# Retention's v, k and y turned by VectorE in 32x32 blocks and put in place by DMA through DRAM, in one layer of a hybrid encoder

## The chip, the core and the metric

The kernel runs on one core of a Trainium2 chip. A core has a tensor engine (PE, with its weight loads shown apart as PEld), VectorE (DVE), ScalarE (ACT), GpSimd (POOL) and SyncE (SP), which issues most transfers, and 16 DMA engines. The metric is the device time of one execution in microseconds, as the median of several runs; less is better.

## The reference

```
h = rms_norm(x)                                  # x: 1024 x 2048, float32
rq, rk, rv, rg, aq, ak, av, ag = split(h @ w_in) # w_in: 2048 x 6656
# retention, 8 heads x 128, per head, in chunks of C = 128 tokens:
q, k = rotary(rq), rotary(rk) * 128**-0.5
scores = (q_c @ k_c.T) * decay                   # within a chunk
inner  = scores @ v_c
kv_c   = (k_c * k_dec).T @ v_c                   # "outer products", 128 x 128
state  = state * chunk_decay + kv_c              # scan over the chunks
cross  = (q_c * q_dec) @ state_before_c
y = inner + cross, forward scan plus backward scan
y = (y - mean) * rsqrt(var + eps) * gn_w + gn_b  # per head, over its 128 columns
y_ret = y * silu(rg)
y_att = window_attention(aq, ak, av) * silu(ag)
out = rms_norm(x + concat(y_ret, y_att) @ w_out)
```

## The kernel before

All of it is float32. The input projection is computed transposed (channels on partitions, tokens along the row) by a two-by-two block scheme with seven products instead of eight, each product a sum of three matmuls on operands split into a high and a low half (lines 98, 99 and 100; matmuls of 128x512). The low half of the weights (`wL`) is made on DVE and the high half (`wH`) on ACT, one product ahead. Finished tiles of 128 channels by 1024 tokens go to DRAM, into `pr`.

The other work runs beside the projection as background jobs: generators that `advance()` moves on by one piece, a step, after every six matmuls of the projection. First attention, then retention head by head, then the gating, beside which the output projection starts. `idle(n)` lets a job rest n steps; `needs` waits until blocks of the projection are done. PE, SP and POOL execute in the order in which the program is written, with this interleaving; the order on DVE and ACT is chosen by a planner.

A retention head: `kT` and `qT` (channels on partitions) are fetched from `pr` with rotary on DVE; scores on PE (line 787); `vT` is fetched (line 761). `transposed()` (line 542) turns a 128x1024 tile by two groups of four 128x128 transposes on PE, each a matmul with `ident`, into PSUM. It is used three times a head: v and k come out as tokens on partitions, copied by ACT to `v_tok` (line 797) and `k_tok` (line 803), and y, normalised on DVE (line 891) with tokens on partitions, is turned back to channels, where ACT multiplies by gn_w and adds gn_b (line 899) before it is stored to `mix` (line 905). `vd` is v scaled by both decays (line 808). The outer products (line 820) take `k_tok` as the stationary and `vd` as the moving operand. The states are split into `sH` and `sL`, 14 pairs of 128x128, for the cross term. The gating loads `mix` and the gate on ACT's queue, three tiles ahead (lines 1280, 1281), and multiplies after Silu.

Stores and small buffers come from rotating pools: `ct` (128x512, 8 buffers), `ax` for results in PSUM. SP's DMAs share eight semaphores, so that at most eight of its transfers are on their way.

Of the kernel before, what the change touches and what calls it, by code (L numbers as in the profile page):

```python
# [17 lines left out]

P = 128
S = 1024  # L20
D = 2048
# [16 lines left out]
M = 4  # L38
# [19 lines left out]
def hybrid_layer_kernel(  # L58
# [80 lines left out]
    pr = [dram.tile([P, S], F32, name=f"pr{i}") for i in range(52)]  # L139
    mix = [dram.tile([P, S], F32, name=f"mix{i}") for i in range(KT)]  # L140

    rows_d = dram.tile([1, HALF], F32, name="rows_d")
# [579 lines left out]


    def retention():
        with right("ret") as ret:
# [4 lines left out]
            busy = set()  # L730
            kq, vs = {}, {}
            rot = ret.tile([P, 2, S], F32, name="rot")
            HP = P // 2

            def fetch(name, c, h):

                t = ret.tile([P, S], F32, name=name, tag=name)
                nc.sync.dma_start(out=t, in_=pr[c + h])
                beside = []

                def pair(i):
                    beside.append(ret.tile([P, HALF], F32, name="rx", tag="sd" if h == 0 and c == T_RQ else "rx", bufs=2))
                    for r in (0, HP):
                        nc.sync.dma_start(out=beside[i][r:r + HP], in_=pr[c + h][HP - r:P - r, half(i)])

                for i in range(2):
                    pair(i)
                yield from idle(7 if h or c == T_RK else 11)
                for i in range(2):
                    u, b = t[:, half(i)], beside[i]  # L750
                    behind(h == 0, nc.vector.tensor_tensor(out=u, in0=u, in1=rot[:, 0, half(i)], op=ALU.mult))
                    yield
                    behind(h == 0, nc.vector.tensor_tensor(out=b, in0=b, in1=rot[:, 1, half(i)], op=ALU.mult))
                    add(u, u, b)
                    yield
                kq[name, h] = t

            def fetch_v(h):
                yield from needs("rv" + str(h // 4))
                t = ret.tile([P, S], F32, name="vT", tag="vdq")  # L760
                nc.sync.dma_start(out=t, in_=pr[T_RV + h])
                yield from idle(5)
                vs[h] = t

            def next_of(name, c, h):
# [6 lines left out]
            def head(h):  # L772
# [10 lines left out]
                for b in range(2):  # L783
                    sc = ax()
                    for t in range(4):
# [5 lines left out]
                                            in1=dT.rearrange("p (o e) -> p o e", o=1).broadcast_to([P, 4, P]), op=ALU.mult)  # L791
                    sds.append(sd)
                while h not in vs:
                    yield
                v = ret.tile([P, NT, P], F32, name="v_tok")
                for b, pt in transposed(vs.pop(h)):
                    nc.scalar.copy(out=v[:, 4 * b:4 * b + 4], in_=chunks(pt))
                    yield
                while busy:
                    yield  # L800
                k_tok = ret.tile([P, NT, P], F32, name="k_tok", tag="y")
                for b, pt in transposed(kT):
                    nc.scalar.copy(out=k_tok[:, 4 * b:4 * b + 4], in_=chunks(pt))
                    yield
                start(next_of("kT", T_RK, h + 1))
                vd = ret.tile([P, NT, 2, P], F32, name="vd", tag="vdq")
                for d in range(2):
                    nc.scalar.mul(vd[:, :, d], v, kd[:, d * RH + h:d * RH + h + 1])
                yield from idle(3)

                sH, sL = (ret.tile([P, 2 * NT - 2, P], F32R, name="s" + c) for c in "HL")
                prev = None
                def outer(i0):
                    kvp = ax()
                    todo = []
                    for i in range(i0, min(i0 + 2, NT - 1)):
                        for d in range(2):
                            c, to = (NT - 1 - i, NT - 2 - i) if d else (i, i + 1)
                            p = kvp[:, blk(len(todo))]
                            nc.tensor.matmul(p, k_tok[:, c], vd[:, c, d], start=True, stop=True)  # L820
                            todo.append((i, d, to, p))
# [4 lines left out]
                for i0 in range(2, NT + 2, 2):  # L826
                    todo, ahead = ahead, (outer(i0) if i0 < NT else None)
                    for i, d, to, p in todo:
# [4 lines left out]
                        else:  # L833
                            nc.vector.scalar_tensor_tensor(out=cur[:, d], in0=prev[:, d], scalar=cd[:, d * RH + h:d * RH + h + 1],  # L834
                                                           in1=p, op0=ALU.mult, op1=ALU.add)
                        split(sH[:, 2 * to + d - 1], sL[:, 2 * to + d - 1], cur[:, d])
                        if d == 1:
                            prev = cur
                    yield
# [9 lines left out]
                def cross(c0):  # L849
                    cr = ax().rearrange("p (c d e) -> p c d e", d=2, e=P)  # L850
                    for t in range(2):
                        c = c0 + t
                        lo, hi = (1 if c == 0 else 0), (1 if c == NT - 1 else 2)
                        mm3(cr[:, t, lo:hi], qH[:, blk(c)], qL[:, blk(c)], *(s[:, 2 * c + lo - 1:2 * c + hi - 1] for s in (sH, sL)))
                    yield
# [8 lines left out]
                def inner(b):  # L864
                    yi = ax()
                    for t in range(4):
                        nc.tensor.matmul(yi[:, blk(t)], sds[b][:, t], v[:, 4 * b + t], start=True, stop=True)  # L867
                    nc.scalar.copy(out=y[:, 4 * b:4 * b + 4], in_=chunks(yi))
# [11 lines left out]
            def normed(h, y, bn, mv):  # L880
# [7 lines left out]
                nc.gpsimd.tensor_tensor(out=rs, in0=rs, in1=neg_half, op=ALU.pow)  # L888
                yield from idle(2)
                for c in range(NT):  # L890
                    nc.vector.tensor_scalar(out=y[:, c], in0=y[:, c], scalar1=mv[:, c, 0:1], scalar2=rs[:, c:c + 1],
                                            op0=ALU.subtract, op1=ALU.mult)
                    if c % 4 == 3:
                        yield
                yield from idle(2)
                outs = []
                for b, pt in transposed(y.rearrange("p c e -> p (c e)")):
                    yo = ct()
                    nc.scalar.activation(out=yo, in_=pt, func=AF.Identity, scale=gw[:, h:h + 1], bias=gb[:, h:h + 1])
                    outs.append((mix[h][:, half(b)], yo))  # L900
                    yield
                busy.discard(h)
                yield
                for dst, yo in outs:
                    nc.sync.dma_start(out=dst, in_=yo)
                finished.add(h)
# [224 lines left out]
    def on_done(p, b):  # L1131
        if b in done:
            since.setdefault(b, clock[0])
        if p == 1 and b == "akv":
            start(attention())
        if p == 2 and b == "rq1":
            start(residual())
# [109 lines left out]
    def gating():  # L1247
# [13 lines left out]
        def operand_tiles(part, gates):  # L1261
# [6 lines left out]
            def mix_in():  # L1268
                d, g = todo.popleft()
                nc.scalar.activation(out=g, in_=g, func=AF.Silu)  # L1270
                nc.vector.tensor_tensor(out=d, in0=d, in1=g, op=ALU.mult)
                mixed.append(d)

            def gate():
                for s in range(2):
                    yield from needs(gates[s])
                    for i in range(s * M, (s + 1) * M):
                        t = (RH if part == 0 else 0) + i
                        d, g = src[:, s, i % M], places[i % 3]
                        behind(True, nc.scalar.dma_start(out=d, in_=mix[t]))  # L1280
                        behind(True, nc.scalar.dma_start(out=g, in_=pr[T_RG + t if t < RH else T_AG + t - RH]))
                        todo.append((d, g))
                        yield
# [243 lines left out]
```

## Time and profile before

| | |
|---|---|
| median of 3 runs | 1525.29 us (1524.96 to 1526.89) |
| profiled execution, span | 1524.4 us (no other time of this execution is recorded) |
| PE / DVE / ACT / POOL busy | 99% / 71% / 45% / 10% |
| DMA moved | 310.53 MB, mean 204 GB/s |
| packets | 153352, of which 13697 under 512 bytes |

The span is from the first to the last recorded instruction. Busy shares are averages over stages of the program; matmuls overlap each other, so a matmul's duration is longer than the distance from one start to the next. In rows of groups, the two numbers behind the bar are the busy time in us and the mean duration of one in ns, and the number behind the next bar is the idle time of the engine just before them, with what ended it. In rows of DMA issues the last numbers are the size and the median time from issue to landing.

### The profile page before, as it was taken

How to read it: one execution, taken by the hardware profiler on the slowest of the kernel's cores; microseconds unless marked ns; L12 is line 12 of the kernel's file. 1: busy time of each engine (PE TensorE's matmuls, PEld its weight loads, DVE VectorE, ACT ScalarE, POOL GpSimd, SP SyncE). 2: the span in 40 equal slices, each digit the busy share in tenths (PEclk: the TensorE clock that was granted, in tenths of full speed). 3: DMA queues.
4: the chain of work that ended last, by engine and by line, in shares of the span. 5: the costliest groups of instructions: out<-in, count | busy, mean ns of one | idle time of the engine just before them, and what ended most of it. 6: DMA issues, size and time to landing. Idle time of an engine off the chain costs nothing.

```text
span 1524.4 us, 20497 instructions
## 1 busy us (share of the span) xinstructions
PE 1510.5 (99%) x7406; PEld 1274.0 (84%) x7406; DVE 1088.3 (71%) x1943; ACT 686.6 (45%) x1139; POOL 151.0 (10%) x169
## 2 busy tenths in 40 slices
PE   9999999999999999999999999999999999999997
PEld 7888888788888888888888888888888888888886
DVE  6896594557767575756977797779755966776766
ACT  7543462234545454533445444543444643542425
POOL 0000001111010000011212000001211102020001
PEclk9999999999999999999999999999999999999999
DMA  8288847889573424796677655488689679395756
GB/s 319 68 277 316 311 166 193 222 207 251 163 204 128 138 80 167 281 315 156 139 179 205 196 174 193 152 297 299 157 207 262 152 217 251 85 212 162 219 177 251
DMA packets 153352, 310.53 MB, mean 204 GB/s; under 512 B 13697, under 2 KB 72481, under 8 KB 144418
## 3 DMA queue, kind: packets, MB, share of 16 engines
q1 hardware_dynamic: 128050, 254.15, 49.1%
q0 software_dynamic: 19728, 36.71, 15.6%
q10 hardware_dynamic: 5472, 18.36, 3.5%
q8 instruction: 58, 0.95, 0.3%
q14 instruction: 44, 0.36, 0.1%
HBM read 193.03 MB, written 124.52 MB: 208 GB/s over the span
## 4 chain that ended last, share of the span: by engine, by line
PE 84%; issue 9%; DMA 4%; DVE 2%; POOL 0%; ACT 0%; SPq 0%; ACTq 0%; POOLq 0%; DVEq 0%
PE pj L100 21%; PE pj L98 21%; PE pj L99 21%; PE ax L99 5%; PE ax L100 5%; PE ax L98 5%; PE ax L820 2%; PE ax L542 1%; DMA xt<-in_x_dram 1%; PE ax L619 1%; DMA pr<-ct 1%; PE ax L787 1%; PE ax L867 1%; DMA yt<-pr 1%; DVE wL L84 0%
## 5 line engine op out<-in xcount | busy, mean ns | idle before, releaser
L98 PE MATMUL pj<-c,wH 128*128 128x512 f32 x1444 | 576.8, 399 | 0.0
L100 PE MATMUL pj<-c,wL 128*128 128x512 f32 x1440 | 562.6, 391 | 1.6 <-DVE wL L84 1.6
L99 PE MATMUL pj<-c,wH 128*128 128x512 f32 x1444 | 563.0, 390 | 0.0
L100 PEld LDWEIGHTS pj<-c,wL 128*128 128x128 f32 x1440 | 270.3, 188 | 60.7 <-DVE wL L84 2.5
L98 PEld LDWEIGHTS pj<-c,wH 128*128 128x128 f32 x1444 | 271.6, 188 | 49.7 <-ACT ct L292 0.4
L99 PEld LDWEIGHTS pj<-c,wH 128*128 128x128 f32 x1444 | 271.8, 188 | 49.5 <-DVE c L948 0.2
L87 ACT CAST wH<-a 128x1024 fp32r<-128x1024 f32 (+1 forms) x159 | 166.3, 1046 | 250.2 <-PE pj L99 138.0
L84 DVE TENSOR_TENSOR wL<-a,wH 128x1024 fp32r<-128x1024 f32 x157 | 191.9, 1222 | 109.4 <-ACT wH L87 105.9
L292 ACT COPY ct<-pj 128x512 f32<-128x512 f32 x192 | 111.1, 584 | 220.3 <-PE pj L100 219.7
L262 POOL DMA_DIRECT2D pr<-ct x104 | 92.2, 961 | 612.9 <-DVE ct L91 474.6
L91 DVE TENSOR_TENSOR ct<-pj,ct 128x512 f32<-128x512 f32 x164 | 109.1, 688 | 58.9 <-PE pj L100 58.0
L84 DVE TENSOR_TENSOR wL<-s,wH 128x1024 fp32r<-128x1024 f32 x56 | 68.4, 1222 | 89.8 <-ACT wH L87 89.4
L99 PE MATMUL pj<-wL,c 128*128 128x512 f32 x224 | 87.3, 390 | 0.0
L100 PE MATMUL pj<-wH,c 128*128 128x512 f32 x224 | 87.2, 389 | 0.0
L98 PE MATMUL pj<-wH,c 128*128 128x512 f32 x224 | 87.1, 389 | 0.0
L99 PE MATMUL ax<-wL,c 128*128 128x512 f32 x208 | 81.2, 390 | 0.4 <-DVE wL L84 0.4
L100 PE MATMUL ax<-wH,c 128*128 128x512 f32 x208 | 80.9, 389 | 0.0
L98 PE MATMUL ax<-wH,c 128*128 128x512 f32 x208 | 80.9, 389 | 0.0
L87 ACT CAST wH<-s 128x1024 fp32r<-128x1024 f32 x56 | 59.1, 1055 | 16.4 <-PE ax L100 8.8
L87 ACT CAST sH<-st 128x128 fp32r<-128x128 f32 x112 | 29.9, 298 | 46.9 <-DVE st L834 29.2
L99 PEld LDWEIGHTS pj<-wL,c 128*128 128x128 f32 x224 | 42.0, 188 | 8.9 <-DVE wL L84 0.3
L98 PEld LDWEIGHTS pj<-wH,c 128*128 128x128 f32 x224 | 42.0, 188 | 8.8
(243 smaller groups left out, 2057.7 us busy)
## 6 DMA issues: line engine op xcount, KB each, us to landing
a<-in_w_in_dram SPq DMA_DIRECT2D x103, 512.0 KB, 5.8
kept<-c SPq DMA_DIRECT2D x28, 1024.0 KB, 7.3
c<-kept SPq DMA_DIRECT2D x28, 1024.0 KB, 9.9
pr<-ct SPq DMA_DIRECT2D x110, 256.0 KB, 5.4
pr<-ct POOLq DMA_DIRECT2D x104, 256.0 KB, 6.2
a<-in_w_out_dram SPq DMA_DIRECT2D x18, 512.0 KB, 5.4
rx<-pr SPq DMA_DIRECT2D x64, 128.0 KB, 3.8
ysrc<-mix ACTq DMA_DIRECT2D x16, 512.0 KB, 5.4
```

Of the source, the lines that this page charges most:

```text
L84: return nc.vector.tensor_tensor(out=dst, in0=src, in1=high.bitcast(F32), op=ALU.subtract)
L87: behind(pinned, nc.scalar.copy(out=dst_h, in_=src))
L91: nc.vector.tensor_tensor(out=dst, in0=a, in1=b, op=ALU.add)
L98: nc.tensor.matmul(po, aH, bH, start=first, stop=False, **kw)
L99: nc.tensor.matmul(po, aH, bL, start=False, stop=False, **kw)
L100: nc.tensor.matmul(po, aL, bH, start=False, stop=last, **kw)
L262: nc.gpsimd.dma_start(out=dst, in_=t, accum_op=ALU.add)
L292: nc.scalar.copy(out=t, in_=bank)
L542: nc.tensor.transpose(pt[:, blk(t)], src[:, blk(b * 4 + t)], ident)
L619: nc.tensor.transpose(pt[:, blk(j)], s[:, blk(j)], ident)
L787: nc.tensor.matmul(sc[:, blk(t)], kT[:, c], qT[:, c], start=True, stop=True)
L820: nc.tensor.matmul(p, k_tok[:, c], vd[:, c, d], start=True, stop=True)
```

## The change

VectorE has a transpose that turns each 32x32 block of a tile in its place. Three helpers use it: `turn_half` (a 128x512 half of v), `turn_pair` (half of y), and a call in the fetch of `kT`. The block positions are put right by a trip through DRAM: the turned tile is stored, and `gather` reads it back by four DMAs of 32 partitions each, in runs of 512 bytes for v (`vz` to `v_tok`), 256 bytes for k (`kz` to `k_tok`) and 1024 bytes for y (`mix`, read in the gating). So:

- v: a job `turn_v`, started after v's projection or one head ahead, loads a half, turns it on DVE and stores it; `fetch_v` gathers. v's columns come in four runs of 32 per chunk, which the later instructions read through an access pattern; `vd` takes four ACT instructions instead of two.
- k: turned after rotary, stored to `kz`, gathered by `fetch_k_tok`. `k_tok` holds two chunks with their columns interleaved, so that the outer product's stationary operand is read with a step of two elements.
- y: normalised by ACT (scale and bias by token) in place of DVE, turned on DVE, stored to `mix`; gn_w and gn_b are applied in the gating, where retention's tiles are gathered by SP.
- apart from this, the states' split takes both directions in one instruction: 7 pairs of 128x256 in place of 14 of 128x128.

```diff
+    def turn_pair(dst, src, pair):
+        nc.vector.transpose(out=dst.rearrange("p (b c i) -> p b c i", b=2, i=SQ),
+                            in_=src.rearrange("p (c b i) -> p b c i", b=NB, i=SQ)[:, 2 * pair:2 * pair + 2])
+    def gather(dst, src):
...
+        for b in range(NB):
+            nc.sync.dma_start(out=dst[b * SQ:(b + 1) * SQ].rearrange("p (n r) -> p n r", r=of.shape[-1]), in_=of[b])
...
+    def turn_v(h):
+        yield from needs("rv" + str(h // 4))
+        for m in range(2):
+            f, z = ct(), ct()
+            nc.sync.dma_start(out=f, in_=pr[T_RV + h][:, half(m)])
+            yield from idle(6)
+            turn_half(z, f)
+            yield
+            nc.sync.dma_start(out=vz[h][m], in_=z)
+            yield
...
+                    if c == T_RK:
+                        zs.append(ct())
+                        for n in range(2):
+                            nc.vector.transpose(out=chunks2(zs[i])[:, n].rearrange("p (b j c) -> p c b j", b=NB, c=2),
+                                                in_=chunks2(u)[:, n].rearrange("p (c b i) -> p c b i", b=NB, c=2))
...
+                start(fetch_k_tok(h))
...
-                for b, pt in transposed(vs.pop(h)):
-                    nc.scalar.copy(out=v[:, 4 * b:4 * b + 4], in_=chunks(pt))
...
-                for b, pt in transposed(kT):
-                    nc.scalar.copy(out=k_tok[:, 4 * b:4 * b + 4], in_=chunks(pt))
...
-                            nc.tensor.matmul(p, k_tok[:, c], vd[:, c, d], start=True, stop=True)
+                            nc.tensor.matmul(p, k_tok[:, c // 2, :, c % 2], vd[:, c, d], start=True, stop=True)
...
-                        split(sH[:, 2 * to + d - 1], sL[:, 2 * to + d - 1], cur[:, d])
                         if d == 1:
+                            both = slice(i, 2 * NT - 2 - i, 2 * NT - 3 - 2 * i)
+                            split(sH[:, both], sL[:, both], cur)
...
-                    nc.vector.tensor_scalar(out=y[:, c], in0=y[:, c], scalar1=mv[:, c, 0:1], scalar2=rs[:, c:c + 1],
-                                            op0=ALU.subtract, op1=ALU.mult)
+                    nc.scalar.activation(out=y[:, c], in_=y[:, c], func=AF.Identity, scale=rs[:, c:c + 1], bias=mv[:, c, 0:1])
...
-                for b, pt in transposed(y.rearrange("p c e -> p (c e)")):
...
+                for b in range(2):
+                    zs.append(ct())
+                    turn_pair(zs[b], y.rearrange("p c e -> p (c e)"), b)
...
+                if t < RH:
+                    nc.scalar.activation(out=e, in_=e, func=AF.Identity, scale=gw[:, t:t + 1], bias=gb[:, t:t + 1])
...
+                        if t < RH:
+                            gather(e, mix[t])
```

The order on PE around the scores of the fourth head (head 3), before: `c` and `wH`, `wL` are the projection's operands, and each row is one instruction or, with x4, four alike.

```order
L787 MATMUL ax<-qT,kT 128x128 x4
L542 MATMUL ax<-ident,y 128x128 x4
L98 MATMUL pj<-c_5644,wH 128x512
L99 MATMUL pj<-c_5644,wH 128x512
L100 MATMUL pj<-c_5644,wL 128x512
L98 MATMUL pj<-c_5644,wH 128x512
L99 MATMUL pj<-c_5644,wH 128x512
L100 MATMUL pj<-c_5644,wL 128x512
L542 MATMUL ax<-ident,vT 128x128 x4
L98 MATMUL pj<-c_5644,wH 128x512
```

And at the same place in the changed kernel (its lines are numbered anew: 99 to 101 are the projection, 850 the scores):

```order
L850 MATMUL ax<-qT,kT 128x128 x4
L99 MATMUL pj<-c_5863,wH 128x512
L100 MATMUL pj<-c_5863,wH 128x512
L101 MATMUL pj<-c_5863,wL 128x512
L99 MATMUL pj<-c_5863,wH 128x512
L100 MATMUL pj<-c_5863,wH 128x512
L101 MATMUL pj<-c_5863,wL 128x512
L850 MATMUL ax<-qT,kT 128x128 x4
L99 MATMUL pj<-c_5863,wH 128x512
```

The two groups with `ident` between the projection's sixes, of y of the head before and of v, are gone; the scores and the sixes stay.

The order on SP from the fetch of qT of head 2 to that of the next kT, before. `a` are weights of the projection, `res` the residual, `mix` the results of head 1.

```order
L738 DMA qT<-pr_67 128x1024
L744 DMA rx<-pr_67 64x512 x4
L1153 DMA res_240<-in_x_dram 16x16384
L761 DMA vT<-pr_83 128x1024
L171 DMA a_7337<-in_w_in_dram 128x4x256
L1153 DMA res_241<-in_x_dram 16x16384
L171 DMA a_7393<-in_w_in_dram 128x4x256
L171 DMA a_7395<-in_w_in_dram 128x4x256
L905 DMA mix_118<-ct 128x512 x2
L738 DMA kT<-pr_76 128x1024
```

The changed kernel, from the same fetch of qT (its `rx`) to the gather of k (`vz_143`, `kz_135`: head 2's v and k on their way through DRAM):

```order
L789 DMA rx<-pr_67 64x512 x4
L765 DMA vz_143<-ct 128x512
L1215 DMA res_257<-in_x_dram 16x16384
L202 DMA a_7307<-in_w_in_dram 128x4x256
L202 DMA a_7309<-in_w_in_dram 128x4x256
L808 DMA kz_135<-ct 128x2x256 x2
L164 DMA v_tok<-vz_143 32x8x128 x4
L202 DMA a_7452<-in_w_in_dram 128x4x256
L965 DMA mix_118<-ct 128x512 x2
L1215 DMA res_258<-in_x_dram 16x16384
L761 DMA ct<-pr_84 128x512
L164 DMA k_tok<-kz_135 32x16x64 x4
```

The load of vT has become loads and stores of halves and a gather of four DMAs, and the store of k and its gather have come in; k's gather stands behind the stores of `mix`, whose data comes from DVE's transpose of y of head 1. In steps of the program: v's gather stands 8 steps ahead of the scaling to `vd` and 5 behind the store of v's second half (in the first head 2 steps behind it), k's gather 9 behind its store and 6 ahead of the outer products. A head takes 27 steps in place of 28, the first outer product of the first head stands 12 steps later, and the gating of retention's part starts 2 steps later.

95 lines of the change are left out of this document (64 added, 31 removed).

## The prediction

> **What bounds the kernel now.** I read first the page's busy times, then the waits of the tensor engine, then the busy times of the stretches with retention in them.
>
> ```profile
> span 1524.4 us, 20497 instructions
> ...
> PE 1510.5 (99%) x7406; PEld 1274.0 (84%) x7406; DVE 1088.3 (71%) x1943; ACT 686.6 (45%) x1139; POOL 151.0 (10%) x169
> ```
>
> PE is busy for 1510.5 of 1524.4 us. This is one profiled execution, whose span lies 0.9 us under the median of the three runs (1525.3), so I add differences to 1525.3. Next, whether PE waits for anything that the change touches:
>
> ```profile
> PE pj L100 <- DVE wL L84: 1.6, 2, 0.9
> PE pj L1086 <- POOL ident masks.py:199: 1.4, 1, 1.4
> ...
> PE ax L99 <- DVE wL L84: 0.4, 1, 0.4
> ```
>
> These are the largest waits of the whole run, with their total, count and longest: under 5 us together, and nothing in them belongs to v, k or y. So PE's own list of work sets the end: work taken from it shortens the run by its full length, as long as the other engines and the transfers keep up with a shorter list. How much room they have shows in two stretches, the middle of retention (four heads long) and the end of it (heads 6 and 7), where the projection also reads its kept input back from DRAM. The columns are window, length, PE, weight loads, DVE, ACT, POOL (each with its instructions), granted clock, DMA share, GB/s:
>
> ```profile
> 801.00:1003.00 202.00, 202.00 (x1104) 173.79 (x1103) 161.14 (x384) 91.69 (x164) 16.68 (x13) 1.00 0.61 186
> 1003.00:1075.00 72.00, 72.00 (x392) 61.70 (x391) 51.81 (x116) 33.61 (x57) 6.10 (x4) 1.00 0.93 324
> ```
>
> A head lasts 202/4 = 50.5 us, with 40.3 us of DVE, 22.9 us of ACT, and DMA at 61%. In the last stretch DMA is at 93%. DVE and, at the end, DMA are what could come next; the clock is 1.00 in both.
>
> **Part 1: 192 transposes leave PE.** The price of one group of four, between the projection's matmuls (start, duration, engine, line):
>
> ```profile
> 760.22 0.39 PE L99 MATMUL pj<-c,wH 128*128 128x512 f32 x1
> 760.44 0.39 PE L100 MATMUL pj<-c,wL 128*128 128x512 f32 x1
> 760.67 0.39 PE L98 MATMUL pj<-c,wH 128*128 128x512 f32 x1
> 760.90 0.39 PE L99 MATMUL pj<-c,wH 128*128 128x512 f32 x1
> 761.12 0.39 PE L100 MATMUL pj<-c,wL 128*128 128x512 f32 x1
> 761.35 0.60 PE L542 MATMUL ax<-ident,vT 128*128 128x128 f32 x4
> 761.71 0.48 PE L98 MATMUL pj<-c,wH 128*128 128x512 f32 x1
> 762.02 0.40 PE L99 MATMUL pj<-c,wH 128*128 128x512 f32 x1
> ```
>
> A step, below, is six matmuls of the projection, after which every side job advances once. Matmuls overlap, so I count from start to start. L100 to the next L99 is two places, 760.44 to 760.90, 0.46 us (0.45 by the mean spacing of 0.226); with the group between, 761.12 to 762.02, it is 0.90. A group costs 0.45 us. Of such groups:
>
> ```profile
> L542 PE MATMUL ax<-ident,y 128*128 128x128 f32 x64 | 9.6, 272 | 0.0
> L542 PE MATMUL ax<-ident,vT 128*128 128x128 f32 x64 | 9.6, 272 | 0.0
> L542 PE MATMUL ax<-ident,kT 128*128 128x128 f32 x64 | 9.6, 272 | 0.0
> ```
>
> 3 × 64 / 4 = 48 groups, 48 × 0.45 = 21.6 us. All other matmuls stay, in number and shape.
>
> **Part 2: VectorE.** Per head it gains two transposes of 128x512 for v, two for y and four of 128x256 columns for k; it loses eight normalisations; the split of the state is done for both directions at once; one 128x8 operation is added. The rows, from the four-head stretch:
>
> ```profile
> L84 DVE TENSOR_TENSOR sL<-st,sH 128x128 fp32r<-128x128 f32 x56 | 14.0, 287 | 0.0
> ...
> L753 DVE TENSOR_TENSOR rx<-rx,rot 128x512 f32<-128x512 f32 x16 | 10.9, 680 | 0.0
> L84 DVE TENSOR_TENSOR wL<-s,wH 128x1024 fp32r<-128x1024 f32 x8 | 9.7, 1218 | 25.1 <-ACT wH L87 25.1
> L891 DVE TENSOR_SCALAR y<-y,mv,rstd 128x128 f32<-128x128 f32 x32 | 9.2, 342 | 1.2 <-POOL rstd L888 1.2
> L887 DVE TENSOR_SCALAR rstd<-mv 128x8 f32<-128x8 f32 x4 | 0.7, 166 | 0.0
> ```
>
> Gone: 8 × 0.342 = 2.7 us. The split: 14 × 0.287 = 4.0 becomes 7 × 0.42 = 2.9 (0.42 lies on the line between 0.287 at 128 and 0.680 at 512 columns), so −1.1. Added 0.17. No transpose of VectorE is in the trace. Lower bound: the 512-column row's time, 0.68, for 4 × 0.68 + 4 × 0.42 = 4.4 us a head; upper bound: twice that, 8.8. I take 4.4, since every pass over 512 columns in this trace takes near 0.68 whatever it computes. DVE has then 40.3 − 2.7 − 1.1 + 0.2 + 4.4 = 41.1 us of work in a head that lasts 50.5 − 6 × 0.45 − 1.36 = 46.4 us (one step of six matmuls shorter in the order, 6 × 0.226 = 1.36): 89%. At twice the price 45.5, or 98%: that is the edge. What hides the work is that DVE was idle for 10 us a head; its critical product is the low half of the weights, which in the tightest place is ready only just in time:
>
> ```profile
> 1059.67 1.22 DVE L84 TENSOR_TENSOR wL<-a,wH 128x1024 fp32r<-128x1024 f32 x1
> 1061.38 0.39 PE L100 MATMUL pj<-c,wL 128*128 128x512 f32 x1
> ```
>
> 1061.38 − (1059.67 + 1.22) = 0.49 us. One transpose of 0.68 in front of such a piece makes PE wait 0.2 us.
>
> The Trainium skill, "VectorE: DVE Perf Modes", section "The three transpose paths", has a rule against this step: VectorE turns only blocks of 32 × 32, so a 128 × 128 transpose belongs on TensorE if its result may lie in PSUM. By it the VectorE way costs extra passes to place the blocks; here these are the DMAs of part 4, and the row says that TensorE has no idle time to give, so by this trace the rule points the wrong way as long as those DMAs stay hidden.
>
> **Part 3: ScalarE.** Per head:
>
> ```profile
> L87 ACT CAST sH<-st 128x128 fp32r<-128x128 f32 x56 | 14.8, 297 | 23.2 <-DVE st L834 14.4 <-DVE st L832 8.8
> L808 ACT ACTIVATE vd<-v_tok,kd 128x1024 f32<-128x1024 f32 x8 | 9.3, 1167 | 0.1
> L899 ACT ACTIVATE ct<-ax,vec_t 128x512 f32<-128x512 f32 x8 | 6.2, 781 | 7.7 <-PE ax L542 7.7
> L803 ACT COPY k_tok<-ax 128x512 f32<-128x512 f32 x8 | 4.8, 600 | 0.0
> L797 ACT COPY v_tok<-ax 128x512 f32<-128x512 f32 x8 | 4.7, 587 | 7.0 <-PE ax L542 7.0
> ```
>
> Gone: 2 × 0.781 + 2 × 0.600 + 2 × 0.587 = 3.9. Split: 14 × 0.297 = 4.2 to 7 × 0.4 = 2.8. vd: 2 × 1.167 to 4 × 0.6. Added: eight normalisations at 0.3, 2.4. Together about −2.8 us in an engine at 45%: worth nothing. In the gating, 8 activations of 128x1024 (1.2 us each) come in, spread over 200 us: also nothing.
>
> **Part 4: the way through DRAM.** Per head SyncE issues 13 DMAs more: v in two halves in and out, k in two halves out, four gathers each of v and k, less one load. Issue time, and the landings nearest in shape:
>
> ```profile
> 818.44 2.40 SPq L744 DMA_DIRECT2D rx<-pr  x4
> ...
> a<-in_w_in_dram SPq DMA_DIRECT2D x16, 512.0 KB, 5.4
> ...
> kT<-pr SPq DMA_DIRECT2D x4, 512.0 KB, 3.8
> ```
>
> 0.6 us each, 8 us of a queue that issues in order. Bytes: 4 × 512 KB = 2.1 MB a head, beside 37.55 MB in those four heads (9.4 a head): in the middle stretch DMA goes from 61% to about 61 × 11.5/9.4 × 50.5/46.4 = 81%. Nothing waits as long as a landing is shorter than the steps left for it. In the program's order the k gather stands 6 steps (8.2 us) ahead of the outer products that read it, the v gather 8 steps (10.9 us) ahead of the scaling by decays. kT has 128 runs of 4 KB and lands in 3.8 us; a has 512 runs of 1 KB, 5.4 us. By bytes alone a 512 KB gather lands in 3.8 us. By count, 384 more runs cost 1.6 us, so v's 1024 runs of 512 bytes take 7.5 and k's 2048 of 256 bytes 11.8. These are the bounds. I take 6 to 8 us, nearer to the bytes: the queues' sum on the page charges 16 × 0.491 × 1524.4 / 128050 = 94 ns for a packet of 1985 bytes and 16 × 0.035 × 1524.4 / 5472 = 156 ns for one of 3355, that is 47 ns per KB in both, with no visible fixed part.
>
> ```profile
> q1 hardware_dynamic: 128050, 254.15, 49.1%
> ...
> q10 hardware_dynamic: 5472, 18.36, 3.5%
> ```
>
> Then the middle heads lose nothing. Two places have less cover. In head 0 v's second half is stored 2 steps (2.7 us) before its gather, and this store's like takes about 5:
>
> ```profile
> mix<-ct SPq DMA_DIRECT2D x8, 256.0 KB, 5.0
> ```
>
> 2.3 us late on SyncE, then 5.4 to 7.5 for the gather, against 10.9: +1 us. The first outer product of head 0 stands 12 steps later in the order than before, but the steps are filled with projection, so this costs nothing by itself. In 1003 to 1075 the same loads take longer:
>
> ```profile
> c<-kept SPq DMA_DIRECT2D x12, 1024.0 KB, 9.9
> ...
> kT<-pr SPq DMA_DIRECT2D x1, 512.0 KB, 8.5
> ...
> vT<-pr SPq DMA_DIRECT2D x1, 512.0 KB, 10.4
> ```
>
> 72/50 heads bring 3 MB more, 9.3 us at 324 GB/s, on DMA that is idle for 5 of the 72. Bound: 0 (the reloads of c are asked for early) to 9.3. PE waited for none of these before, so I take 2.
>
> The gating reads retention's half by 32 gathers on SyncE in place of 8 loads on ScalarE's queue, 2 steps later than before; each has several steps until it is multiplied, and PE then computes the output projection of other halves: 0, at most the 3 to 5 us of a late first one.
>
> **Sum.** −21.6 + 1 + 2 = −18.6; 1525.3 − 18.6 = 1506.7 us.
>
> **Rivals.**
> Second bound: DVE at the doubled price, or DMA in the last heads at its upper end. 89% becomes 98%, weights' low halves come late by a few tenths of a us per product, some 28 products in retention, and the last heads lose up to 9: 5 to 15 us back, 1512 to 1522. For it: the 0.49 us place. Against: of the 41 us that DVE was idle in the four heads, 25.1 ended with ScalarE's cast of a product's weights (the wL row of part 2), so DVE was there ahead of its input and not behind.
>
> The step-2 read: k_tok is the stationary operand of the outer products, and now its columns lie 8 bytes apart. If reading at that step doubles a pass, at most their whole busy time comes on top:
>
> ```profile
> L820 PE MATMUL ax<-vd,k_tok 128*128 128x128 f32 x224 | 30.2, 275 | 0.0
> ```
>
> 30.2 us, less what overlaps: 1522 to 1537, with the gain eaten. Against: nothing in the trace reads at a step. The Trainium skill, "SBUF — State Buffer", section "Door 1: The DMA port swizzle", holds that 16-byte lines want two accesses each, so that a step of two fp32 elements would still be free; no run shows it yet.
>
> The other side: the gather of k by its count of runs. If 2048 runs of 256 bytes land in 11.8 us, PE waits 11.8 − 8.2 = 3.6 us in six heads, and in the two last, with landings 6 us longer, 9.6 each: 41 us, 1506.7 + 41 − 3 = 1545. It decides from a landing of 8.2 us plus what PE saves in a head (2.7), so slower than before from 10.9 on. For it: the 4-KB and 1-KB loads differ by 1.6 us. Against: 47 ns per KB. The Trainium skill, "DMA: Bandwidth & Descriptors", in its first table puts the line rate at 512 bytes and more, with a read-modify-write below, which favours this rival for k alone; no packet row of the trace is grouped by such a size.
>
> **How the numbers follow.** First case, 1502 to 1512: 0.62. Second bound, 1512 to 1522: 0.18. Step-2 read, 1522 to 1537: 0.06. Late k gather, above 1528: 0.10. Other ways to be slower: 0.04. What three runs can tell from no change is 0.2%, 3 us. Faster 0.80, same 0.06 (half of the step-2 case and the border of the others), slower 0.14. The range, 1501 to 1522, takes in the first two cases: 0.8.
>
> **What would show it.** No transposes of y, vT and kT on PE, and PE busy near 1489 (1510.5 − 21.6). DVE's transposes at 0.6 to 0.7 us for 512 columns. Outer products at 275 ns as before: above 300, the step-2 rival. Landing of k_tok's gathers: 6 to 8 us, with PE's waits free of k_tok and vd; 11 or more, with such waits, means the last rival. DMA near 80% in the middle. PE waits for wL above 5 us in total: the second case. I am wrong if PE's waits sum to over 10 us, whichever engine they name.

## The result and the profile after

The changed kernel takes 1559.97 us (median; 1557.96 to 1567.17) against 1525.12 us before on the same chip: 1.0232 times as long, 95% interval 1.0212 to 1.0251. The forecast of 1506.7 us was 53 us off and on the wrong side.

The page's first rows of the changed kernel:

```profile
span 1556.2 us, 20272 instructions
...
PE 1503.3 (97%) x7214; PEld 1261.2 (81%) x7214; DVE 1101.9 (71%) x1895; ACT 686.3 (44%) x1123; POOL 150.4 (10%) x169
```

The span grew by 31.8 us. Three numbers make that up. The 21.6 us of transposes (by the price of part 1) are gone. PE's idle time rose from 1524.4 − 1510.5 = 13.9 to 1556.2 − 1503.3 = 52.9, by 39.0. And the rest of PE's work, 1510.5 − 21.6 = 1488.9 by the old prices, took 1503.3, 14.4 more. −21.6 + 39.0 + 14.4 = 31.8. What PE waited for (line of the waiting matmul, what released it, total, times, longest; L881 is the outer product, L99 to L101 the projection):

```profile
PE ax L881 <- DMA k_tok<-kz: 23.0, 6, 10.3
PE ax L881 <- ACT vd L865: 4.4, 2, 3.1
PE pj L99 <- DMA c<-kept: 3.8, 1, 3.8
PE pj L101 <- DVE wL L85: 3.2, 5, 0.9
PE pj L100 <- DMA c<-kept: 3.0, 1, 3.0
```

More than half is the gather of k. All rows of this view sum to 43.8 us, against 4.2 before. The two stretches read before (the same times; the work in them has shifted somewhat):

```profile
801.00:1003.00 202.00, 192.88 (x1002) 164.53 (x1001) 168.58 (x369) 87.93 (x155) 16.61 (x12) 0.98 0.78 229
1003.00:1075.00 72.00, 60.06 (x311) 51.37 (x310) 50.82 (x106) 25.05 (x43) 4.34 (x3) 0.91 0.89 279
```

DMA in the middle went from 61% to 78%, and PE's clock, 1.00 before, has 0.98 and 0.91 in these stretches. One late head (head 2) in full. SyncE's issues (start, time of the whole row, line, transfer), then PE's rows:

```profile
829.54 0.39 SPq L202 DMA_DIRECT2D a<-in_w_in_dram  x1
829.98 0.98 SPq L965 DMA_DIRECT2D mix<-ct  x2
831.00 0.52 SPq L1215 DMA_DIRECT2D res<-in_x_dram  x1
831.63 1.39 SPq L761 DMA_DIRECT2D ct<-pr  x1
833.07 7.61 SPq L164 DMA_DIRECT2D k_tok<-kz  x4
```

```profile
838.55 0.39 PE L101 MATMUL pj<-c,wL 128*128 128x512 f32 x1
846.80 2.05 PE L881 MATMUL ax<-vd,k_tok 128*128 128x128 f32 x8 [7.87 <-DMA k_tok<-kz]
848.50 0.77 PE L99 MATMUL pj<-c,wH 128*128 128x512 f32 x1
849.08 0.63 PE L100 MATMUL pj<-c,wH 128*128 128x512 f32 x1
849.50 0.63 PE L101 MATMUL pj<-c,wL 128*128 128x512 f32 x1
```

PE reached the outer products at 838.8. The gather had been issued from 833.07 on, 5.7 us ahead and not 8.2, its four issues took 7.61 us and not 2.4, and the last piece landed at 846.7. After the wait, matmuls start 0.42 us apart (849.08 to 849.50) in place of 0.23, for the clock is halved:

```profile
846.70:850.20 3.50, 3.40 (x12) 3.14 (x13) 1.63 (x6) 0.68 (x2) 0.00 (x0) 0.50 1.28 392
```

So a wait of 7.9 us costs, as an estimate from these 3.5 us at 0.50, some 1.7 us more behind it.

Why SyncE came late to the gather stands on ScalarE and VectorE:

```profile
823.88 3.19 ACT L955 ACTIVATE y<-y,mv,rstd 128x128 f32<-128x128 f32 x8 [6.22 <-DVE mv L952]
826.98 1.03 ACT L88 CAST wH<-a 128x1024 fp32r<-128x1024 f32 x1
```

```profile
827.10 1.31 DVE L148 STREAM_TRANSPOSE ct<-y 128x512 f32<-128x512 f32 x2 [1.52 <-ACT y L955]
828.33 1.18 DVE L85 TENSOR_TENSOR wL<-a,wH 128x1024 fp32r<-128x1024 f32 x1
```

From 821.8 on SyncE stood at the load of `a`, whose buffer is free once VectorE has made a low half `wL`. That low half stood behind y's normalisation on ScalarE and behind y's transposes on VectorE, was done at 829.5, and only then came the load of `a`, the stores of `mix`, the residual, v's load and the gather. In heads 3 and 4 SyncE stood 6.4 and 4.8 us at the same load, released in the same way. SyncE waits for `wL` in the kernel before too; new is that k's gather stands behind such a wait.

What else was on its way: the stretches of three gathers of k, from first issue to last landing, in heads 2, 3 and 6 (columns as in the rows of stretches above; the packets' times overlap in the records, so that DMA's share can pass 1). Below them is the queue of GpSimd's transfers in the first stretch, with packets, MB and share of the 16 engines' time:

```profile
833.07:846.67 13.60, 5.87 (x26) 4.51 (x25) 5.83 (x8) 2.34 (x4) 1.73 (x2) 0.89 1.12 293
888.45:894.62 6.17, 6.17 (x29) 5.12 (x28) 2.86 (x4) 2.22 (x4) 0.00 (x0) 1.00 1.10 303
1034.33:1048.31 13.98, 4.74 (x21) 3.57 (x20) 3.32 (x5) 3.52 (x5) 0.00 (x0) 0.76 1.07 311
```

```profile
q0 software_dynamic: 571, 1.04, 42.2%
```

The DMA engines were full in all three, also in head 3, where the gather was on its way for 6.2 us only. What differs is how much had to pass through them. In head 2 GpSimd's accumulating stores of the projection (`pr<-ct`) took 42.2% of 13.6 us, that is 5.7 us of all 16 engines; they took 4.9 us in the gather of head 1, 5.7 in that of head 7, and none in the others. In head 6 4.35 MB moved during the gather, two reloads `c<-kept` of 1 MB among them, against 1.87 MB in head 3.

The issue and landing records of all eight gathers of k, put together (us; "time given" is from the first issue to PE's arrival at the outer product, "needed" from the first issue to the last landing on record):

| head | time given | needed | PE's wait |
|---|---|---|---|
| 0 | 26.1 | 7.3 | 3.2 (for vd) |
| 1 | 8.3 | 9.6 | 1.5 |
| 2 | 5.7 | 13.6 | 8.0 |
| 3 | 6.8 | 6.2 | 0 |
| 4 | 6.1 | 6.3 | 0.8 |
| 5 | 6.4 | 6.9 | 0.6 |
| 6 | 4.6 | 14.0 | 10.5 |
| 7 | 16.3 | 18.9 | 2.8 |

### The profile page after: what moved, and what is told of

Read it like the earlier page. It is cut to its first block, busy times and chain, and to the rows that moved or that the text cites. A ratio compares the mean times of both kernels' runs of the same rounds, so it can differ in the third digit from the quotient of the medians.

```text
span 1556.2 us, 20272 instructions
## 1 busy us (share of the span) xinstructions
PE 1503.3 (97%) x7214; PEld 1261.2 (81%) x7214; DVE 1101.9 (71%) x1895; ACT 686.3 (44%) x1123; POOL 150.4 (10%) x169
## 4 chain that ended last, share of the span: by engine, by line
PE 61%; DMA 15%; issue 10%; DVE 7%; SPq 3%; ACT 1%; POOL 1%; ACTq 0%; POOLq 0%; DVEq 0%
PE pj L101 15%; PE pj L100 15%; PE pj L99 15%; PE ax L100 4%; PE ax L101 4%; PE ax L99 4%; DMA ysrc<-pr 3%; DMA k_tok<-kz 2%; SPq L164 2%; DVE wL L85 2%; DMA pr<-ct 2%; PE ax L881 2%; DMA xt<-in_x_dram 1%; DMA v_tok<-vz 1%; PE ax L650 1%
## 5 line engine op out<-in xcount | busy, mean ns | idle before, releaser
L99 PE MATMUL pj<-c,wH 128*128 128x512 f32 x1444 | 576.2, 399 | 4.7 <-DMA c<-kept 3.8
L101 PE MATMUL pj<-c,wL 128*128 128x512 f32 x1440 | 564.8, 392 | 3.3 <-DVE wL L85 3.2
L101 PEld LDWEIGHTS pj<-c,wL 128*128 128x128 f32 x1440 | 271.6, 189 | 64.5 <-DVE wL L85 6.8
L99 PEld LDWEIGHTS pj<-c,wH 128*128 128x128 f32 x1444 | 272.9, 189 | 56.4 <-issue 4.2
L99 PE MATMUL pj<-wH,c 128*128 128x512 f32 x224 | 87.3, 390 | 1.0 <-ACT wH L88 1.0
L101 PE MATMUL pj<-wH,c 128*128 128x512 f32 x224 | 87.2, 389 | 0.0
L99 PE MATMUL ax<-wH,c 128*128 128x512 f32 x208 | 81.0, 389 | 0.0
L101 PE MATMUL ax<-wH,c 128*128 128x512 f32 x208 | 80.9, 389 | 0.0
L881 PE MATMUL ax<-vd,k_tok 128*128 128x128 f32 x224 | 35.2, 302 | 27.4 <-DMA k_tok<-kz 23.0
L881 PEld LDWEIGHTS ax<-vd,k_tok 128*128 128x128 f32 x224 | 33.7, 213 | 32.7 <-issue 24.8
L88 ACT CAST sH<-st 128x256 fp32r<-128x256 f32 x56 | 22.6, 406 | 84.7 <-DVE st L893 61.6
```

The source lines that it names most:

```text
L88: behind(pinned, nc.scalar.copy(out=dst_h, in_=src))
L99: nc.tensor.matmul(po, aH, bH, start=first, stop=False, **kw)
L101: nc.tensor.matmul(po, aL, bH, start=False, stop=last, **kw)
L881: nc.tensor.matmul(p, k_tok[:, c // 2, :, c % 2], vd[:, c, d], start=True, stop=True)
```

## The experiments

Theory A: k's gather is late because the time given to it is too short for transfers that share full DMA engines; the stalls and the half clock behind them are the loss. Called A2 later, it says that what fills the engines in heads 6 and 7 is their own time, of which the way through DRAM takes more than was free. Rival B: the 2048 small pieces make the gather long. Rival C: VectorE and ScalarE are late by themselves. D, E and F are named where they come up. All ratios are to the kernel before on the same chip.

**k on TensorE again.** The edit:

```diff
-                start(fetch_k_tok(h))
...
+                k_tok = ret.tile([P, NT, P], F32, name="k_tok", tag="y")
+                for b, pt in transposed(kT):
+                    nc.scalar.copy(out=k_tok[:, 4 * b:4 * b + 4], in_=chunks(pt))
```

> k alone goes back to TensorE: two groups of four transposes a head and ScalarE's copies, no store and no gather of k; v and y stay as changed. Theory A (k's gather lands too late, since its 8.2 us are filled with other transfers): the 23.0 us of PE's waits for k_tok<-kz and most of the slow-clock time behind them go, the waits for c<-kept (6.8 us) shrink, 16 groups x 0.45 = 7.2 us come back: 1515 to 1525 us. Rival C (the loss is VectorE's and SyncE's load as a whole, k's waits only show it): PE waits as long for something else, 1545 or more.

1528.8 us, 1.0016 (1.0006 to 1.0026). 31 us come back, the waits for k and c are gone and vd's is 0.4 us; but by the sum it should stand 14.4 us below the kernel before on this chip, at 1526.3 − 14.4 = 1511.9. What PE waits for now:

```profile
PE pj L101 <- DVE wL L85: 4.5, 6, 1.0
PE ax L99 <- ACT sH L88: 2.4, 2, 1.5
```

15.9 us in all against 4.2 before, in pieces of about 1 us, none for a transfer. One of them, in time order (VectorE, then PE):

```profile
779.79 1.31 DVE L148 STREAM_TRANSPOSE ct<-y 128x512 f32<-128x512 f32 x2 [1.52 <-ACT y L953]
781.02 1.18 DVE L85 TENSOR_TENSOR wL<-a,wH 128x1024 fp32r<-128x1024 f32 x1
```

```profile
782.26 0.50 PE L101 MATMUL pj<-c,wL 128*128 128x512 f32 x1 [0.78 <-DVE wL L85]
```

VectorE stood idle 1.52 us for ScalarE's normalised y, then turned it, and only then made the low half that the projection was about to read. A's share is the 31 us. Of the other 17, 11.7 are longer waits, which fit C. The rest is that PE was busy 1502.1 us in place of 1510.5 − 14.4 = 1496.1; a stretch of 3.4 us at half the clock accounts for 1.7 of these 6.0, and what makes the others is open.

**v on TensorE again.**

```diff
-        if p == 2 and b == "rv0":
-            start(turn_v(0))
...
-                gather(t, vz[h])
+                nc.sync.dma_start(out=t, in_=pr[T_RV + h])
```

> v alone goes back to TensorE; k and y stay as changed. Theory A: 1 MB less per head is on its way around k's gather, and the loads and stores of v next to it in SyncE's queue are gone, so PE's waits for k_tok fall from 23 us to some 10 but do not vanish; vd's 4.4 us go; 7.2 us of transposes come back: 1535 to 1548 us. If the waits for k_tok stay at 20 us or more, v's transfers are not what k's gather meets: 1553 or more.

1539.7 us, 1.0082 (1.0056 to 1.0108), as theory A has it. vd's wait goes and k's is halved:

```profile
PE ax L879 <- DMA k_tok<-kz: 12.3, 4, 5.5
```

The gathers of heads 2, 6 and 7 now need 8.4, 10.6 and 13.2 us in place of 13.6, 14.0 and 18.9. That v's transfers are part of what k's gather meets is not shown by this alone: every head also stands 14 steps earlier, and GpSimd's stores take 1.4 us of the engines in head 2's gather in place of 5.7.

**y on TensorE again.**

```diff
-                    nc.scalar.activation(out=y[:, c], in_=y[:, c], func=AF.Identity, scale=rs[:, c:c + 1], bias=mv[:, c, 0:1])
+                    nc.vector.tensor_scalar(out=y[:, c], in0=y[:, c], scalar1=mv[:, c, 0:1], scalar2=rs[:, c:c + 1], ...
...
-                    turn_pair(zs[b], y.rearrange("p c e -> p (c e)"), b)
+                for b, pt in transposed(y.rearrange("p c e -> p (c e)")):
```

> y alone goes back: normalised on VectorE, turned on TensorE, gn_w and gn_b by ScalarE before the store, the gating loads on ScalarE's queue. k and v stay as changed. Theory A: y brought no transfers near k's gather, so the waits for k_tok stay near 23 us and 7.2 us come back: 1560 to 1570 us. If y's longer way to the mix stores holds up SyncE ahead of k's gather, the waits fall below 12 us: 1550 or less.

1536.0 us, 1.0064 (1.0049 to 1.0079): a miss of 24 us against what I expected of theory A. The expectation's other branch came, in which y's way holds up SyncE ahead of k's gather.

```profile
PE ax L881 <- ACT vd L865: 5.8, 2, 4.4
PE ax L881 <- DMA k_tok<-kz: 4.5, 2, 3.5
```

The records tell why. In heads 1 to 5 the gather now has 9.1 to 9.5 us given, and needs 3.5 to 10.4; in head 6 it has 7.0 and needs 10.5. In the program the gather still stands 6 steps ahead, but SyncE no longer comes late to it in heads 1 to 5. That fits the rows of head 2 above: y's transposes no longer stand ahead of the low halves for which SyncE's list waits. GpSimd's stores are still in the way (4.7 us of the engines in head 2), and head 2's gather needs 9.1 us, but it has 9.1. The time given was the other half of theory A, and I had sized only the landing.

**The same bytes in larger pieces.** This kernel leaves out the placing of k's blocks, so its result is not the layer's; it serves for the time alone.

```diff
-                gather(t, kz[h])
+                for b in range(NB):
+                    rows = slice(b * SQ, (b + 1) * SQ)
+                    nc.sync.dma_start(out=t[rows].rearrange("p (c e) -> p c e", c=M),
+                                      in_=kz[h][:, rows].rearrange("c p b r -> p c (b r)"))
```

> As changed, but k's gather reads the same 512 KB at the same place in the order, by four DMAs again, in 512 runs of 1 KB that leave the blocks where they are; so the blocks of k are not put in place. Theory A (crowding): the DMA engines' time of the gather falls from 3.0 us (2048 packets at 24 ns over 16 engines) to 1.5, so each late head gains about 1.5 us and as much again in the slow clock: waits for k_tok 14 to 18 us, 1545 to 1552 us. Rival B (the count of pieces makes it late): waits for k_tok under 5 us, 1530 or less.

1553.8 us, 1.0181 (1.0162 to 1.0201).

```profile
PE ax L883 <- DMA k_tok<-kz: 25.7, 4, 17.9
```

Rival B falls. With a quarter of the pieces the gathers of heads 1 to 6 need 9.4, 12.3, 6.2, 6.0, 5.6 and 14.4 us, all within 1.3 us of the 256-byte ones. The four issues take 2.2 us in place of 7.6 in head 2 and 3.7 in place of 13.2 in head 7, and the last landing comes hardly sooner (12.3 and 18.3 us in place of 13.6 and 18.9), so the long issue was not what made the gather late. The small gain that A gave it (waits of 14 to 18 us) did not come either: in head 6 SyncE issued the gather 3.0 us after PE had come, and that wait grew from 10.5 to 17.9 us.

**k's gather earlier.** Counted in the program, the edit moves it by 2 steps, from 6 to 8 ahead of the outer products (2.7 us), and not by the 3 that are expected below: a job that is started is moved on once more in the same step, so that the step taken out had cost none.

```diff
                 kT, qT = kq.pop(("kT", h)), kq.pop(("qT", h))
+                start(fetch_k_tok(h))
...
                 gather(t, kz[h])
-                yield from idle(5)
+                yield from idle(8)
```

> As changed, but k's gather is issued 3 steps (4.1 us) earlier, as soon as y's buffer is free and ahead of the stores of mix; the outer products stay at their step. Theory A (the gather had 4.6 to 8.3 us until PE came, and needs 6.2 us where the DMA engines have room, 9.6 to 14 where not): waits for k_tok 4 to 10 us instead of 23, heads 3 to 5 without any, 1535 to 1545 us. Rival D (in the crowded heads the gather only moves to the queue's end, behind the same transfers, and lands as late as before): waits for k_tok 18 us or more, 1553 or more.

1550.3 us, 1.0163 (1.0144 to 1.0182), between the two theories.

```profile
PE ax L880 <- DMA k_tok<-kz: 12.5, 3, 10.4
PE pj L99 <- DMA c<-kept: 5.3, 1, 5.3
```

Head 2's wait falls from 8.0 to 1.9 us and head 1's from 1.5 to 0. Head 6 keeps 10.5: with 8 steps in the program the gather had 4.3 us there, since SyncE, whose list waits for landings of 10 us and more, reached it that much later. Rival D is right for head 6 and wrong for the others.

**The first head's v halves together.**

```diff
+        for m in range(2):
+            fs.append(ct())
+            nc.sync.dma_start(out=fs[m], in_=pr[T_RV + h][:, half(m)])
+            if h:
+                yield from idle(3)
...
+        for m in range(2):
+            z = ct()
+            turn_half(z, fs[m])
```

> As changed, but the first head's two halves of v are loaded together and turned one after the other, so that its gather stands 6 steps earlier against its stores; the first outer product stands 6 steps earlier too. Theory A: PE's wait of 3.2 to 4.6 us at the first outer product with the half clock behind it goes or is halved, the later heads stay: 1553 to 1560 us. If the shift of all heads against the projection's own transfers matters (crowding at other heads), the later waits change by more than 5 us, in either direction.

1557.7 us, 1.0211 (1.0196 to 1.0227). PE's waits for vd fall from 4.4 to 1.3 us, but the waits for k rise to 30.4 (head 7 waits 15.8 us in place of 2.8, and c<-kept none). The gain is spent elsewhere. All heads stand 6 steps earlier against the projection's own transfers; the edit also loads the second half of v 3 steps after the first, in place of 8, in the other heads, and which of the two moved the waits was not separated.

**All three on TensorE; of the change only the joint split is left.** The three edits above together.

> v, k and y all go back to TensorE; of the change there is left the states' split of both directions in one instruction, 7 of 128x256 for 14 of 128x128. Theory A: nothing to do with the loss, 1524 to 1528 us. Rival E (the joint split makes the states late for the cross term, which cost the kernel with k alone undone part of its 17 us): PE waits for sH and sL over 4 us, 1530 or more.

1527.2 us, 1.0012 (1.0003 to 1.0021); waits sum to 4.6 us, 0.2 of them for sL. Rival E falls.

**y alone through VectorE.** The edits for k and v together.

> y alone turned by VectorE, and the joint split; v and k on TensorE. By the sum of the prediction 16 groups x 0.45 = 7.2 us less, the gathers in the gating hidden: 1518 us. If y's way itself costs (ScalarE's normalisation or the gathers in the gating), 1524 or more with waits of PE for other engines above 8 us.

1525.6 us, 0.9995 (0.9978 to 1.0012): no difference shown. PE is busy 1505.8 us, 4.7 less than before, at the same mean clock of 0.998; its waits are 8.5 us, 4.3 more. The 7.2 us that the sum gave are not seen in the time.

**v and k on TensorE in heads 6 and 7 only.**

```diff
-                    if c == T_RK:
+                    if c == T_RK and not (h >= 6):
...
+                if h >= 6:
...
+                    for b, pt in transposed(vs.pop(h)):
...
+                    for b, pt in transposed(kT):
```

> As changed in heads 0 to 5; in heads 6 and 7 v and k are turned on TensorE as before (8 groups x 0.45 = 3.6 us), y stays on VectorE. Theory A2 (in the last heads the DMA engines had 5 us of 72 free, and the way through DRAM brings 8 us of their time per head: 1 MB in 2-KB packets, 512- and 256-byte packets): the stalls at heads 6 and 7 and the waits for c<-kept go, together 20 us of waits and the half clock behind them: 1534 to 1543 us; heads 0 to 2 keep theirs (13 us). Rival F (SyncE's long list in all heads is the cause, and it makes up later what it lost early): c or k waits of 10 us or more stay after 1000 us, 1550 or more.

1544.5 us, 1.0121 (1.0104 to 1.0138), 1.5 us above what A2 gave. No wait for k, v or c after 1000 us is left; of those before:

```profile
PE ax L910 <- DMA k_tok<-kz: 9.1, 2, 7.7
```

Head 2 still waits 7.9 us. Rival F falls: what happens at the end is of those heads' own making.

**k's gather issued by ScalarE.**

```diff
-                gather(t, kz[h])
+                for b in range(NB):
+                    behind(True, nc.scalar.dma_start(out=..., in_=of[b]))
```

> As changed, but the four gathers of k are issued by ScalarE, at about the same place, so they neither stand behind SyncE's list nor take its slots. Theory A2 (engine time): the gathers still land 9 to 14 us after their issue in heads 1, 2, 6 and 7, waits for k_tok 15 us or more, 1550 to 1562 us. Rival F (SyncE's queue holds them up: in head 6 it came 3.6 us late and took 9.2 us to issue four): waits for k_tok under 8 us, 1540 or less.

1585.9 us, 1.0393 (1.0374 to 1.0413), worse than either theory said.

```profile
PE ax L883 <- DMA k_tok<-kz: 41.5, 5, 14.3
```

The gathers need 9.0 to 20.4 us, also in heads 3 to 5 (12.0, 10.6, 11.2), and in heads 2 and 4 to 7 they are issued later against PE than from SyncE (in head 6, 0.9 us after PE came), in heads 0, 1 and 3 earlier. Taking them off SyncE's list does not free them. Why they need longer on the other queue is not settled.

**The three remedies together:** k's gather 2 steps earlier, the first head's halves together, heads 6 and 7 on TensorE.

> Heads 0 to 5 as changed with k's gather 3 steps earlier and the first head's halves of v loaded together; heads 6 and 7 with v and k on TensorE. Theory A2: the three sources of waits are treated, 40 groups of 48 stay off PE (18 us), some 8 to 10 us of waits remain (head 2, late low halves of weights): 1514 to 1520 us, faster than both kernels. Rival C (VectorE and ScalarE are late by themselves with this work, as the 17 us lost with k alone undone suggest): 1525 or more, with waits for wL, sL and sH above 10 us.

1528.5 us, 1.0009 (0.9995 to 1.0022). Every wait for k, and for c, is gone: given 8.4 to 9.9 us, the gathers of heads 1 to 5 need 4.2 to 7.8. Still there:

```profile
PE pj L101 <- DVE wL L85: 3.8, 7, 0.9
PE ax L864 <- DVE qT L92: 3.3, 3, 1.5
PE ax L101 <- DVE qhl L85: 1.5, 1, 1.5
```

17.9 us in all, of many small kinds, against 4.2 before; 1.2 of them are for a transfer (`xt`). 18 us of transposes less bought nothing. Rival C gave the time; of its sign only a part came, since the waits for wL, sL and sH sum to 7.9 us and not to more than 10.

**v alone through VectorE,** with the first head's halves together.

> v alone goes through VectorE and DRAM (512-byte pieces), the first head's halves loaded together; k and y on TensorE, y normalised on VectorE as before, and the joint split of the states. v's gather has 8 steps until it is read, so no wait for v, vd or c. By the sum: 16 groups x 0.45 = 7.2 us less: 1517 to 1520 us, faster than both kernels. Rival C (two transposes of 0.7 us a head in VectorE's fixed order are enough to make low halves late): waits of PE for wL, sL and sH of 6 us or more, 1524 or more.

1541.3 us, 1.0093 (1.0076 to 1.0110): 23 us above the sum. No wait is for a transfer; the longest is one of 4.7 us for the states:

```profile
PE ax L99 <- ACT sH L88: 6.1, 3, 4.7
PE pj L101 <- DVE wL L85: 4.8, 6, 1.2
```

Around it, on VectorE and ScalarE:

```profile
856.17 1.21 DVE L85 TENSOR_TENSOR wL<-s,wH 128x1024 fp32r<-128x1024 f32 x1
...
857.64 0.59 DVE L901 SCALAR_TENSOR_TENSOR st<-st,cd,ax 128x128 f32<-128x128 f32 x2
858.16 0.70 DVE L153 STREAM_TRANSPOSE ct<-ct 128x512 f32<-128x512 f32 x1
858.79 0.30 DVE L901 SCALAR_TENSOR_TENSOR st<-st,cd,ax 128x128 f32<-128x128 f32 x1
```

```profile
858.27 0.40 ACT L88 CAST sH<-st 128x256 fp32r<-128x256 f32 x1 [1.09 <-DVE st L901]
859.71 0.41 ACT L88 CAST sH<-st 128x256 fp32r<-128x256 f32 x1 [1.04 <-DVE st L901]
```

The states are a chain of steps on VectorE, each followed by ScalarE's cast. The transpose of v stands between two of these steps, as a low half of weights does just before, and ScalarE idles about 1 us each time; PE, which is ready for the cross term at 855.5, gets its states at 860.2. Whether the added 8 us of work or the new order among old work does this was not separated.

## Why the prediction was wrong

- **Part 1, PE's saving:** the 192 transposes are gone (7406 matmuls to 7214). But with y alone turned, a third of them, PE was busy 4.7 us less and not 7.2, at the same clock. The other 2.5 us are open.
- **Part 2, VectorE's price:** right, and not the edge it was feared to be. 128x512 takes 0.69 to 0.71 us (0.68 taken), 128x256 columns of k 0.42, 34.4 us in all or 4.3 a head (4.4 taken):

```profile
L803 DVE STREAM_TRANSPOSE ct<-kT 128x256 f32<-128x256 f32 x32 | 12.7, 420 | 0.0
L153 DVE STREAM_TRANSPOSE ct<-ct 128x512 f32<-128x512 f32 x16 | 11.3, 705 | 26.0 <-DMA ct<-pr 26.0
L148 DVE STREAM_TRANSPOSE ct<-y 128x512 f32<-128x512 f32 x16 | 10.4, 690 | 9.9 <-ACT y L955 9.9
```

  The step that failed here is "89%, so it is hidden". VectorE executes in a fixed order: work that waits for its own input (26.0 and 9.9 us of idle time in these rows) holds up the low halves and states behind it. The kernel with k on TensorE stands some 17 us above its sum and the combined one some 20, with hardly a wait of PE for a transfer; the waits by themselves are 11.7 and 13.7 us longer than before. The same step failed in part 3, "worth nothing": y's eight normalisations stand ahead of a high half of weights (823.88 and 826.98 in head 2). The guess of 0.68 us had luck in it: passes over 512 columns took 0.48 to 0.75 us in the trace before, and not always near 0.68.
- **Part 4, "the middle heads lose nothing":** the failed step with most of the loss. The landing was sized from typical loads and not from what would be on its way at each gather. Where neither GpSimd's accumulating stores nor reloads of c came in between, it was right: 6.2 to 6.9 us in heads 3 to 5, 6 to 8 taken. In heads 1, 2, 6 and 7 it was 9.6 to 18.9. The other side of the comparison, 8.2 us given, was read from the order of the program; on the chip it was 4.6 to 6.8 in heads 2 to 6, since SyncE arrived late, in heads 2 to 4 behind a low half that stood behind y's transposes.
- **The term "2 us" for the last heads:** mis-sized. It came out at 10.5 us (head 6), 2.8 (head 7) and 6.8 for c<-kept, 20 with the half clock left out. My upper bound of 9.3 counted bytes at the stretch's rate, on DMA that was 93% full already.
- **The term "1 us" for head 0:** 4.4 us were measured, in two waits for vd. The store of v's second half was issued at 727.0 and landed at 731.5, and its gather at 738.7. By the bounds given there (2.3 + 5.4 to 7.5, against 10.9) the term should have been 0; the gather took 7.1 us, within them, and what came late was the turning and storing of the half.
- **No term at all:** the clock. Behind the longest waits PE ran at half speed for 3.4 us (head 0) to 5.9 us (head 6). In all the stretches at half clock between 741 and 1110 PE was busy 18.5 us, which is 9.2 of the 14.4 us by which its remaining work grew; the step-2 read below is 1.1, and some 4 are open.
- **The rivals:** "the other side" was the one that happened, k's gather later than the outer product, but not by its count of pieces, which the 1-KB run excludes, and not in every head. It had 0.10. The second bound was right in its late low halves and in the last heads, though not by a doubled price, and by itself large enough to eat the gain. The step-2 read is excluded. Before and after, eight passes of outer product and the next matmul's start:

```profile
823.36 1.06 PE L820 MATMUL ax<-vd,k_tok 128*128 128x128 f32 x8
824.17 0.48 PE L98 MATMUL pj<-c,wH 128*128 128x512 f32 x1
```

```profile
895.21 1.09 PE L881 MATMUL ax<-vd,k_tok 128*128 128x128 f32 x8
896.06 0.48 PE L99 MATMUL pj<-c,wH 128*128 128x512 f32 x1
```

  0.81 against 0.85 us, 1.1 us over 28 such groups and not 30. The mean duration rose from 275 to 302 ns, over the mark of 300 that I had set for this rival, but through the passes at half clock: the median is 281. The Trainium skill, "SBUF — State Buffer", "Door 1: The DMA port swizzle", says that a step of two fp32 elements within a 16-byte line is free; by these rows it is nearly so.

The Trainium skill's rule on 128 × 128 transposes ("VectorE: DVE Perf Modes", "Rules for kernel authors"), which I set aside since TensorE had no idle time, gave the right advice here, at 1559.97 against 1525.12 us: the blocks' way to their places was not hidden.

## What to carry to other kernels

A transfer in a static order is hidden only if the time from when its queue really issues it to when it is needed is longer than its landing in that very stretch; read both from the stretch, with the queue's own lateness, and count what else passes through the DMA engines there, in engine time and over all queues. Their busy share alone does not tell it: it was 1.10 where the gather landed in 6.2 us and 1.12 where it took 13.6. Work moved from the bounding engine to one with idle time is paid for where it stands in that engine's order: look at what comes right behind it, and at which queue waits for that. And a wait of several microseconds on TensorE costs more than its length.

## What was not expected of the hardware

- After a wait of 7.9 us the granted clock was 0.50 for 3.5 us; in the whole run the mean fell from 0.998 to 0.987. The Trainium skill, "TensorE: Matmul & The Clock Gate", Part 1, tells of a gate with a window of about 3.4 us that halves the clock after idle time; the trace agrees.
- The four issues of a gather took 2.0 us in head 5 and 7.6, 9.2 and 13.2 us in heads 2, 6 and 7; in 1-KB runs, with a quarter of the pieces, they took 1.8, 2.2, 5.0 and 3.7 us at the same places.
- A packet of 256 bytes occupies a DMA engine 18 ns (median), one of 512 bytes 27 and one of 1024 bytes 46; the smallest cost half as much again per byte, yet the gather in 1-KB runs landed at most 1.3 us sooner in heads 1 to 6. GpSimd's accumulating stores took 178 ns for 2048 bytes, transfers of that size in the hardware queue 84.
